# Feed-forward projections of a diffusion block: two plain matrix products against one Strassen level each

## The chip, the cores and the metric

One core of a Trainium2 chip (trn2) runs the whole layer as one program. The metric is device time in microseconds (us) of one execution, as the median of several runs. PE is the matmul engine (TensorE), DVE the vector engine, ACT the scalar engine, POOL is GpSimd, and SP is the engine whose queue issues most transfers.

## The reference

The layer mixes 1024 tokens of width 1024 (retention, Fourier mixing, gates) and ends in a gated feed-forward network with a width-3 depthwise convolution over the tokens, which is what changes here:

```python
x = x + g1 * y
h2 = modulate(rms_norm(x, norm2_w[layer]), sh2, sc2)
x = x + g2 * conv_ffn(h2, w_up[layer], conv_w[layer], conv_b[layer], w_down[layer])
...
def conv_ffn(h, w_up, conv_w, conv_b, w_down):
    u = depthwise_conv3(h @ w_up, conv_w, conv_b)
    a, val = jnp.split(u, 2, axis=-1)
    return (jax.nn.gelu(a) * val) @ w_down
```

`w_up` is 1024 x 5632, `w_down` 2816 x 1024, and all is float32; the result is `rms_norm(x, final_norm_w)`.

## The kernel before

Every large float32 product is done as three fast ones: `split` (L93) copies an operand rounded to the matmul's format into a "hi" tile on ACT and takes the rest into a "lo" tile with a subtraction on DVE, and `mm3` (L111) adds hi*hi, lo*hi and hi*lo (L112 to L114) into one PSUM tile. A PE instruction multiplies a 128 x 128 block by a 128 x 512 block.

The stage ahead of the feed-forward network takes tokens in two halves t = 0, 1 of 512. For each it makes `re` (retention projection, merged with the gates into `y`), then `wo` (output projection; two column halves i, four token blocks n), adds to the residual `acc`, sums squares on ACT (`sum_sq`, L740), takes the reciprocal root on POOL (`rms_rstd`, L743), and turns `acc` by PE transposes (L810) into `h2` with the features on the partitions. A small matmul `rb` (L804) spreads the root over the partitions; DVE scales the transposes with it.

The feed-forward loop runs over NF = 22 blocks i of 128 channels. Each loads its piece of `w_up` (`wload_k`), makes the two tiles `u` (gate and value, j = 0, 1) over all tokens with 2 x 2 x 8 x 3 = 96 matmuls, convolves (one ACT pass, L867, and two DVE passes of 1023 columns), applies gelu (L874), multiplies, and splits the product into `p`. After each second block `down(q)` multiplies that `p` by 256 rows of `w_down`, 96 matmuls again, and DVE adds the result to `acc` (L49). The last `down` also normalises and stores the output, token block by token block. `acc` stays in SBUF all through.

The order on each engine is not the program's order: the framework schedules it when the program is built (`schedule_with_timeline_sim=True`), and each engine then runs its list in that order, waiting where an operand is not there. Loads are issued by SP. PSUM has four kinds of tiles, of which `rt` and `mmt` hand out the ones used here.

Of the kernel before, what the change touches and what calls it, by code (L numbers as in the profile page):

```python
# [16 lines left out]
P = 128  # L17
# [8 lines left out]
NF = FF // P  # L26
EPS = 1e-6
# [15 lines left out]
def tile_block(ctx: ExitStack, tc: tile.TileContext, a: dict, out: bass.AP):  # L43
# [19 lines left out]
    wp = ctx.enter_context(tc.tile_pool(name="wp", bufs=2))  # L63
    ap = ctx.enter_context(tc.tile_pool(name="ap", bufs=4))
# [62 lines left out]
    pr = [ctx.enter_context(tc.tile_pool(name="pr0", bufs=2, space=PSUM))]  # L127
# [221 lines left out]
    with tc.tile_pool(name="rp", bufs=1) as rp:  # L349
# [173 lines left out]
        pm.append(ctx.enter_context(tc.tile_pool(name="pm", bufs=2, space=PSUM)))  # L523
        pr.append(ctx.enter_context(tc.tile_pool(name="pr1", bufs=2, space=PSUM)))
# [227 lines left out]
    with tc.tile_pool(name="mp", bufs=2) as mp, tc.tile_pool(name="bp", bufs=2) as bp:  # L752
        g1 = mp.tile([P, L], F32, tag="g1", bufs=1, name="g1")
        dma(g1, g_d[0].partition_broadcast(P))

        r = load_r(0)
        for t in range(2):
            y = tuple((ap if t == 0 else bp).tile([P, KD, 512], F32R, tag="A" if t == 0 else "B", name=f"y{t}{n}")
                      for n in "hl")
            for i in range(4):  # L760
                w = wload_k(a["w_ret"], i, f"wr{t}")
                sr = mp.tile([P, 2, 512], F32, tag="xn", bufs=4, name=f"sr{t}{i}")
                tf = mp.tile([P, 2, 512], F32, tag="xn", bufs=4, name=f"tf{t}{i}")
# [3 lines left out]
                ps = mmt(f"re{t}{i}").rearrange("p (m n) -> p m n", m=2)  # L767
                for j in range(2):
                    for k in range(KD):
                        mm3(ps[:, j, :], pick(w, ALL, k, blk(j)), pick(r, ALL, k), k == 0, k == KD - 1)  # L770
                for j in (slice(0, 2),) if i < 3 else (slice(0, 1), slice(1, 2)):
                    tt(sr[:, j], sr[:, j], ps[:, j], MUL)
                    tt(sr[:, j], sr[:, j], tf[:, j], ADD)
                    ys = slice(2 * i + j.start, 2 * i + j.stop)
                    split(y[0][:, ys, :], y[1][:, ys, :], sr[:, j])
            for n in range(4):
                dma(acc[t][:, n, :], a["xn"][4 * t + n])
            for i in range(2):
                pns = [rt(f"wo{t}{i}{n}") for n in range(4)]
                for q in range(2):  # L780
                    w = wload_k(a["w_out"], 2 * i + q, f"wo{t}{q}", 4)
                    for n in range(4):
                        for k in range(4):
                            mm3(pns[n], pick(y, ALL, 4 * q + k, blk(n)), pick(w, ALL, k), k + q == 0, k + q == 4)
                if t == 0 and i == 1:
                    r = load_r(1)
                if i == 1:
                    sqs = [ssq(f"b{t}{n}") for n in range(4)]
                    junk = mp.tile([P, L], F32, tag="xn", bufs=4, name=f"junk{t}")
                    for n in range(4):  # L790
# [8 lines left out]
            h2.append(tuple(ap.tile([P, KD, 512], F32R, tag="A", name=f"h2{t}{n}") for n in "hl"))
            dg = mp.tile([P, 4, P], F32, tag="dg", bufs=1, name=f"dg{t}")  # L800
            for n in range(4):
                tsc(dg[:, n, :], ident, rms_rstd(sqs[n]), MUL)
            ps = rt(f"rb{t}")
            T.matmul(ps, ones[:, 0:128], dg.rearrange("p n c -> p (n c)"), start=True, stop=True)  # L804
            rb = mp.tile([P, 512], F32, tag="rb", bufs=1, name=f"rb{t}")
            S.copy(rb, ps)
            for k in range(KD):
                ps = rt(f"tr{t}{k}")
                for n in range(4):
                    T.transpose(out=ps[:, blk(n)], in_=acc[t][:, n, blk(k)], identity=ident)  # L810
                hf = mp.tile([P, 512], F32, tag="rraw", bufs=2, name=f"h2f{t}{k}")
                hi, lo = h2[t][0][:, k, :], h2[t][1][:, k, :]
                stt(hf, ps, a2[:, k:k + 1], rb, MUL, MUL)
                S.activation(hi, hf, AF.Identity, bias=b2[:, k:k + 1])
                stt(lo, hf, b2[:, k:k + 1], hi.bitcast(F32), ADD, SUB)

    with tc.tile_pool(name="ff", bufs=2) as ff:
        g2 = ff.tile([P, L], F32, tag="g2", bufs=1, name="g2")
        fnw = ff.tile([P, L], F32, tag="fnw", bufs=1, name="fnw")
        dma(g2, g_d[1].partition_broadcast(P))  # L820
        dma(fnw, a["fnw"].partition_broadcast(P))
        pts = []

        def down(q):
            last = q == NF // 2 - 1
            w = wload_k(a["w_down"], q, "wd", 2, scale=g2)
            for n in range(NT):
# [22 lines left out]
        for i in range(NF):  # L850
# [28 lines left out]
            if i % 2 == 1:  # L879
                pts.append(pt)  # L880
                if i > 1:
                    down(i // 2 - 1)
# [113 lines left out]
```

## Time and profile before

| | |
|---|---|
| median of 3 runs | 1619.82 us (1619.3 to 1620.79) |
| the profiled execution: span, first to last instruction | 1617.7 us |
| PE busy | 1597.0 us (99%), 8206 instructions |
| DVE busy | 893.0 us (55%), 1556 instructions |
| ACT busy | 473.3 us (29%) |
| POOL busy | 33.9 us (2%) |
| transfers | 152.87 MB, mean 94 GB/s |

The profiled execution is known by its span alone, which is 2.1 us under the median of the runs; that difference is what lies around it. The `re` matmuls start at 705.8 us, the first `u` matmul at 884.6 us, and the last `down` matmul at 1607.0 us.

### The profile page before, as it was taken

The page shows a single profiled execution, that of the slowest core. Times are in us where ns is not written, and L with a number is a line of the kernel's source. Part 1 is how long each engine was busy: PE and PEld are TensorE (multiplying, and loading weights), DVE is VectorE, ACT ScalarE, POOL GpSimd, SP SyncE. Part 2 cuts the span into 40 slices and gives each one's busy share as a digit, 9 for nine tenths or more (in the row PEclk, how much of TensorE's full clock was granted, in tenths as well). Part 3 has the DMA queues.
Part 4 walks back from the last instruction along what each step waited for, and adds up shares of the span by engine and source line. Part 5 has one row for each costly group of instructions (what it writes and reads, how often), then busy time and mean ns, then how long its engine had stood idle before and what let it go on. Part 6 is the DMA issues. An engine that isn't in the chain of part 4 may idle for free.

```text
span 1617.7 us, 19863 instructions
## 1 busy us (share of the span) xinstructions
PE 1597.0 (99%) x8206; PEld 1344.2 (83%) x8206; DVE 893.0 (55%) x1556; ACT 473.3 (29%) x715; POOL 33.9 (2%) x40
## 2 busy tenths in 40 slices
PE   7999999999999999999999999999999999999997
PEld 4789989898888888888888888888888888888886
DVE  5586739476642642135675655555465454554656
ACT  6563131232412231122433431221212212212123
POOL 0000000000000000000000000000000000000002
PEclk9999999999999999999999999999999999999999
DMA  9234121123443322185542211110111102011102
GB/s 357 98 134 158 59 98 55 70 85 131 141 146 113 119 66 73 46 309 172 183 156 88 69 52 51 54 51 28 52 53 52 53 29 75 32 47 53 52 13 105
DMA packets 51019, 152.87 MB, mean 94 GB/s; under 512 B 6241, under 2 KB 10609, under 8 KB 50929
## 3 DMA queue, kind: packets, MB, share of 16 engines
q1 hardware_dynamic: 50928, 151.61, 27.5%
q8 instruction: 64, 1.05, 0.3%
q14 instruction: 27, 0.21, 0.0%
HBM read 134.77 MB, written 16.79 MB: 94 GB/s over the span
## 4 chain that ended last, share of the span: by engine, by line
PE 95%; DVE 3%; DMA 1%; ACT 0%; issue 0%; SPq 0%; DVEq 0%; POOLq 0%; POOL 0%
PE u L113 10%; PE u L114 10%; PE u L112 10%; PE d L114 5%; PE d L113 5%; PE d L112 5%; PE gr L114 2%; PE g L114 2%; PE gr L112 2%; PE re L112 2%; PE gr L113 2%; PE gf L112 2%; PE re L114 2%; PE re L113 2%; PE gf L114 2%; PE gf L113 2%
## 5 line engine op out<-in xcount | busy, mean ns | idle before, releaser
L49 DVE TENSOR_TENSOR acc<-acc,d 128x512 f32<-128x512 f32 x176 | 118.6, 683 | 89.1 <-PE d L114 88.5
L58 DVE SCALAR_TENSOR_TENSOR t<-u,convw,t 128x1023 f32<-128x1023 f32 (+2 forms) x90 | 112.8, 1255 | 36.7 <-ACT t L867 35.6
L175 DVE SCALAR_TENSOR_TENSOR mt<-mt,silrow 128x512 f32<-128x512 f32 x64 | 41.7, 688 | 58.3 <-DMA mt<-wmT 58.2
L867 ACT ACTIVATE t<-u,convb,convw 128x1024 f32<-128x1024 f32 (+1 forms) x45 | 53.3, 1187 | 61.9 <-PE u L114 61.9
L491 ACT ACTIVATE on<-o,nm,rst 128x128 f32<-128x128 f32 x64 | 24.0, 456 | 90.3 <-DVE nm L58 90.3
L874 ACT ACTIVATE t<-t 128x1024 f32<-128x1024 f32 x22 | 23.3, 1060 | 69.4 <-DVE t L58 69.4
L49 DVE TENSOR_TENSOR s<-s,fo 128x1024 f32<-128x1024 f32 x8 | 9.8, 1220 | 54.9 <-PE fo L114 43.0
L58 DVE SCALAR_TENSOR_TENSOR ss<-ss,sm,kv 64x128 f32<-64x128 f32 x112 | 38.0, 346 | 3.0
L484 DVE BATCH_NORM_STATS2 st<-o 128x6 f32<-128x128 f32 x64 | 14.2, 284 | 36.3 <-PE o L477 36.3
L49 DVE TENSOR_TENSOR rr<-ot,sg 128x512 f32<-128x512 f32 x16 | 11.0, 688 | 33.6 <-PE ot L495 33.6
L487 POOL TENSOR_TENSOR rst<-rst,mhalf 128x4 f32<-128x4 f32 x16 | 17.3, 1081 | 491.2 <-DVE rst L53 491.2
L49 DVE TENSOR_TENSOR t<-t,t 128x1024 f32<-128x1024 f32 x22 | 26.9, 1221 | 0.4
L476 PE MATMUL o<-v,pt 128*128 128x128 f32 x128 | 24.8, 275 | 0.0
L477 PE MATMUL o<-ss,qfb 128*128 128x128 f32 x128 | 24.7, 275 | 0.0
L561 ACT COPY qkr<-qk 128x1024 f32<-128x1024 f32 x6 | 6.1, 1014 | 57.7 <-PE qk L114 57.7
L583 ACT ACTIVATE s<-gf,bbg 128x1024 f32<-128x1024 f32 x8 | 8.9, 1113 | 46.5 <-PE gf L114 46.5
L49 DVE TENSOR_TENSOR sr<-sr,re 128x1024 f32<-128x1024 f32 (+1 forms) x10 | 9.9, 1006 | 22.4 <-PE re L114 18.0
L49 DVE TENSOR_TENSOR ro<-qkr,ropec 128x512 f32<-128x512 f32 x32 | 20.8, 682 | 1.6 <-ACT qkr L561 0.9
L476 PEld LDWEIGHTS o<-v,pt 128*128 128x128 f32 x128 | 20.1, 191 | 0.9
L49 DVE TENSOR_TENSOR qfb<-qT,tab 64x1024 f32<-64x1024 f32 x16 | 19.5, 1219 | 0.2
L58 DVE SCALAR_TENSOR_TENSOR ek<-ek,er 128x512 f32<-128x512 f32 (+2 forms) x36 | 19.0, 526 | 0.9
L477 PEld LDWEIGHTS o<-ss,qfb 128*128 128x128 f32 x128 | 19.4, 192 | 0.0
(1208 smaller groups left out, 5069.7 us busy)
## 6 DMA issues: line engine op xcount, KB each, us to landing
mt<-wmT SPq DMA_DIRECT2D x32, 512.0 KB, 3.3
xh<-xT SPq DMA_DIRECT2D x8, 512.0 KB, 7.4
r_d<-rr SPq DMA_DIRECT2D x16, 256.0 KB, 3.3
sr_d<-sr SPq DMA_DIRECT2D x8, 512.0 KB, 4.0
t_d<-s SPq DMA_DIRECT2D x8, 512.0 KB, 2.6
rraw<-r_d SPq DMA_DIRECT2D x8, 512.0 KB, 4.3
acc<-xn SPq DMA_DIRECT2D x8, 512.0 KB, 9.1
sr<-sr_d SPq DMA_DIRECT2D x8, 512.0 KB, 5.6
```

Source lines behind the costliest of these rows:

```text
L49: V.tensor_tensor(out=out, in0=in0, in1=in1, op=op)
L58: V.scalar_tensor_tensor(out=out, in0=in0, scalar=s, in1=in1, op0=op0, op1=op1)
L112: T.matmul(o, l[0], r[0], start=first, stop=False)
L113: T.matmul(o, l[0], r[1], start=False, stop=False)
L114: T.matmul(o, l[1], r[0], start=False, stop=last)
L175: V.scalar_tensor_tensor(out=raw[:, c], in0=raw[:, c], scalar=1.0, in1=silrow[:, c], op0=MUL, op1=MUL, accum_out=acc[:, h:h + 1])
L476: T.matmul(o[:, blk(n)], pt[:, n, :], vt[t][:, n, blk(i)], start=True, stop=False)
L477: T.matmul(o[:, blk(n)], qfb[i][:, blk(4 * t + n)], ss[i][:, 4 * t + n, :], start=False, stop=True)
L487: G.tensor_tensor(out=rs, in0=rs, in1=mhalf, op=ALU.pow)
L491: S.activation(on[:, n, :], o[:, blk(n)], AF.Identity, bias=nm[:, n:n + 1], scale=rs[:, n:n + 1])
L867: S.activation(tl[:, o:o + n], ps, AF.Identity, bias=convb[:, c:c + 1], scale=convw[:, c, 1:2])
L874: S.activation(u[0], u[0], AF.Gelu_apprx_tanh)
```

## The change

Each of the two projections becomes one level of Strassen's scheme (in Winograd's form): the operands are cut in 2 x 2 blocks, and seven block products with sums of blocks take the place of eight. For the up projection the blocks are token halves and feature halves of `h2` (`hops`: a11, a12, a22 and the sums s1 to s4) and of the weights (`wops`: b11, b21, b22 and the sums t1 to t4); for each i, `chain` makes a product of 12 matmuls. Products that share a sum add up in one PSUM tile (`x`, `y`, `z`), with copies to `ca`, `cv` in between. The gated product of two channel blocks j and j + 11 goes through four more sums (`sums`) and is stored to DRAM by transfers that POOL issues, seven of 256 KB for each pair. When all is up, the down projection reads them back: seven products of 11 steps, in each of which both operands are split and 12 matmuls done. `x` after the first residual goes to DRAM as well (`x2_d`) and comes back at the end. PSUM becomes one pool of eight tiles.

The core of the diff (the `wo` code around it is reordered, too):

```diff
+    def chain(ps, x, y, first):
+        for k in range(4):
+            for l, r in ((0, 0), (0, 1), (1, 0)):
+                T.matmul(ps, x[:, l, k], y[:, r, k], start=(first and k == 0 and l + r == 0), ...)
+    def wop(i, name, src):
+        t = fw.tile([P, 2, 4, P], F32R, tag="op", bufs=8, name=f"w{name}{i}")
+        split(t[:, 0], t[:, 1], src)
+    def up_first(i):
+        bank[i, "x"], bank[i, "z"] = rt(f"x{i}"), rt(f"z{i}")
+        chain(bank[i, "x"], wops[i, "b11"], hops["a11"], True)
+        chain(bank[i, "z"], wops[i, "b21"], hops["a12"], True)
...
+        def hops_out(t, n):
...
+                h1, s12 = xn(f"h1{n}", (KD, P)), xn(f"s12{n}", (2, 4, P))
+                dma(h1, h_d[n].rearrange("p (k c) -> p k c", k=KD))
+                s1, s2, s3, s4 = s12[:, 0], s12[:, 1], h1[:, 0:4], h1[:, 4:8]
+                tt(s3, s3, lo, SUB)
+                tt(s2, hi, s3, SUB)
+                hop("s2", s2)
+                tt(s1, lo, hi, ADD)
+                hop("s1", s1)
+                hop("s3", s3)
+                tt(s4, s4, s2, SUB)
+                hop("s4", s4)
+                hop("a22", hi)
...
+        def up_mm(i):
...
+            S.copy(ca[:, lo], x)
+            tt(ca[:, lo], ca[:, lo], z, ADD)
+            chain(x, wops[i, "t2"], hops["s2"], False)
+            S.copy(cv[:, lo], x)
+            chain(y, wops[i, "t1"], hops["s1"], True)
+            S.copy(cv[:, hi], y)
+            chain(x, wops[i, "t3"], hops["s3"], False)
+            tt(cv[:, hi], cv[:, hi], x, ADD)
+            chain(y, wops[i, "b22"], hops["s4"], False)
+            tt(cv[:, lo], cv[:, lo], y, ADD)
+            chain(x, wops[i, "t4"], hops["a22"], False)
+            S.copy(ca[:, hi], x)
...
+        def sums(j, pa, pb):
+            A11, A21, A12, A22 = pa[:, 0:512], pa[:, 512:], pb[:, 0:512], pb[:, 512:]
+            G.dma_start(p_d[0][j], A11)
+            G.dma_start(p_d[1][j], A12)
+            G.dma_start(p_d[6][j], A22)
+            s1, s2, s3 = (ff.tile([P, 512], F32, tag="s", bufs=2, name=f"s{q}_{j}") for q in range(1, 4))
+            tt(s1, A21, A22, ADD)
+            G.dma_start(p_d[3][j], s1)
+            tt(s2, s1, A11, SUB)
+            G.dma_start(p_d[2][j], s2)
+            tt(s3, A11, A21, SUB)
+            G.dma_start(p_d[4][j], s3)
+            tt(A12, A12, s2, SUB)
+            G.dma_start(p_d[5][j], A12)
...
+        for k in K:
+            step(Y, a_op(5, k), dop("ob", f"ob5{k}", raws[3, k]), False, N4)
```

On every engine the order is the same as before up to the `re` matmuls. After them it differs in three places that matter below.

PE, at the start of the feed-forward network. Before (`u` tiles of the first channel block; `rb1`, `tr1k` belong to the second token half):

```order
L112 MATMUL u01_7548<-h20h_6731,wu0hi_7485 128x512
L113 MATMUL u01_7548<-h20l_6732,wu0hi_7485 128x512
L114 MATMUL u01_7548<-h20h_6731,wu0lo_7486 128x512
L112 MATMUL u01_7548<-h20h_6731,wu0hi_7485 128x512
L804 MATMUL rb1_7400<-dg1_7383,ones_84 128x512
L810 MATMUL tr11_7413<-ident_66,acc1_6131 128x128 x4
L113 MATMUL u01_7548<-h20l_6732,wu0hi_7485 128x512
L114 MATMUL u01_7548<-h20h_6731,wu0lo_7486 128x512
L112 MATMUL u01_7548<-h20h_6731,wu0hi_7485 128x512
```

Now (`wb` and `wt` are weight operands, `trNM` transposes of token block N):

```order
L774 MATMUL z0_7686<-a12_6721,wb210_7490 128x512 x10
L774 MATMUL z1_7738<-a12_6721,wb211_7646 128x512 x2
L774 MATMUL x11_7711<-a11_6720,wb1111_7565 128x512 x10
L774 MATMUL z11_7712<-a12_6721,wb2111_7568 128x512 x10
L774 MATMUL x1_7737<-a11_6720,wb111_7643 128x512 x10
L774 MATMUL z1_7738<-a12_6721,wb211_7646 128x512 x10
L826 MATMUL tr130_7764<-ident_66,xr13_7636 128x128 x4
L826 MATMUL tr131_7773<-ident_66,xr13_7636 128x128 x4
L774 MATMUL x0_7685<-s2_7412,wt20_7811 128x512 x2
L774 MATMUL y0_7828<-s1_7413,wt10_7814 128x512 x2
L774 MATMUL x0_7685<-s2_7412,wt20_7811 128x512 x10
L774 MATMUL y0_7828<-s1_7413,wt10_7814 128x512 x10
```

Before, 48 matmuls on the first token half (`h20`) stood around `rb1` and the transposes. Now the 72 matmuls of `x`, `z` of three blocks stand ahead of the last transposes `tr130`, `tr131`, and what follows needs `s2`, `s1` of all tokens and `wt20`.

DVE at the same place. Before (`dg` makes the root's diagonal, `h21l` is the second half's lo part):

```order
L53 TENSOR_SCALAR dg1_7383<-ident_66,ssqb12_7358 128x128 [waits Pool_49]
L49 TENSOR_TENSOR wu1lo_7608<-wu1r1_7613,wu1hi_7607 128x1024 [waits DMAHW4_49,Activation_49]
L49 TENSOR_TENSOR ssqb13_7359<-ssqb13_7359 128x1 [waits Activation_49]
L55 TENSOR_SCALAR ssqb13_7359<-ssqb13_7359 128x1 [waits DVE_49]
L53 TENSOR_SCALAR dg1_7383<-ident_66,ssqb13_7359 128x128 [waits Pool_49]
L58 SCALAR_TENSOR_TENSOR h2f10_7409<-tr10_7404,a2_78,rb1_7402 128x512 [waits Activation_49]
L58 SCALAR_TENSOR_TENSOR h2f11_7418<-tr11_7413,a2_78,rb1_7402 128x512 [waits PE_49]
L58 SCALAR_TENSOR_TENSOR h21l_7382<-h2f10_7409,modc_72,h21h_7381 128x512 [waits Activation_49]
L58 SCALAR_TENSOR_TENSOR h21l_7382<-h2f11_7418,modc_72,h21h_7381 128x512 [waits Activation_49]
```

Now (`s123`, `h13` are the sums of the last token block, `t1_0` to `t4_0` the weight sums of block 0):

```order
L50 TENSOR_TENSOR s123_7783<-hv13_7763,h13_7782 128x512 [waits DVE_49]
L50 TENSOR_TENSOR s1_7413<-s123_7783,s1_7413 128x4x128 [waits Activation_49]
L50 TENSOR_TENSOR s3_7414<-h13_7782,s3_7414 128x4x128 [waits Activation_49]
L50 TENSOR_TENSOR h13_7782<-h13_7782,s123_7783 128x512 [waits DVE_49]
L50 TENSOR_TENSOR s2_7412<-s123_7783,s2_7412 128x4x128 [waits Activation_49]
L50 TENSOR_TENSOR s4_7415<-h13_7782,s4_7415 128x4x128 [waits Activation_49]
L50 TENSOR_TENSOR t1_0_7805<-u0r1_7803,u0r0_7485 128x512 [waits DMAHW2_49]
L50 TENSOR_TENSOR ca0_7829<-ca0_7829,z0_7686 128x512 [waits Activation_49]
L50 TENSOR_TENSOR t2_0_7806<-u0r1_7803,t1_0_7805 128x512 [waits DVE_49]
L50 TENSOR_TENSOR t3_0_7807<-u0r1_7803 128x512
L50 TENSOR_TENSOR t4_0_7808<-u0r0_7485,t2_0_7806 128x512 [waits DVE_49]
L50 TENSOR_TENSOR wt20_7811<-t2_0_7806,wt20_7811 128x512 [waits Activation_49]
```

From the first column scaling of `hv10` to `wt20` there are 72 DVE instructions: 52 of 512 columns, 16 of 128 columns and 4 of one column. Two scalings and two subtractions for each of eight feature blocks stood in their place.

DVE at the end of the up loop. Before (the last gated product beside `down`'s additions):

```order
L49 TENSOR_TENSOR t210_11350<-t210_11350,t211_11403 128x1024 [waits DVE_49]
L49 TENSOR_TENSOR acc0_6130<-acc0_6130,d930_11471 128x512 [waits PE_49]
L49 TENSOR_TENSOR acc0_6130<-acc0_6130,d931_11479 128x512 [waits PE_49]
L49 TENSOR_TENSOR p20l_11288<-t210_11350,p20h_11287 128x1024 [waits Activation_49]
L49 TENSOR_TENSOR acc1_6131<-acc1_6131,d940_11487 128x512 [waits PE_49]
L49 TENSOR_TENSOR acc1_6131<-acc1_6131,d941_11495 128x512 [waits PE_49]
L49 TENSOR_TENSOR acc1_6131<-acc1_6131,d950_11503 128x512 [waits PE_49]
```

Now (`t210`, `t211` are the last block's tiles, `oa04`, `ob04` the first operands of the down products that are not prepared ahead), and under it ACT at the same place:

```order
L59 SCALAR_TENSOR_TENSOR t210_10913<-ca21_10822,convw_80,t210_10913 128x1023 [waits DMASW7_49,Activation_49]
L59 SCALAR_TENSOR_TENSOR t211_10917<-cv21_10823,convw_80,t211_10917 128x1023 [waits DMASW4_49,DMASW1_49,Activation_49]
L59 SCALAR_TENSOR_TENSOR t210_10913<-ca21_10822,convw_80,t210_10913 128x1023 [waits DVE_49]
L59 SCALAR_TENSOR_TENSOR t211_10917<-cv21_10823,convw_80,t211_10917 128x1023 [waits DVE_49]
L50 TENSOR_TENSOR t210_10913<-t210_10913,t211_10917 128x1024 [waits DVE_49,Activation_49]
L50 TENSOR_TENSOR s1_10_10926<-t100_10811,t210_10913 128x512 [waits DMASW3_49,DVE_49]
L50 TENSOR_TENSOR s2_10_10927<-s1_10_10926,t100_10811 128x512 [waits DMASW5_49,DVE_49]
L50 TENSOR_TENSOR t210_10913<-t210_10913,s2_10_10927 128x512 [waits DMASW7_49,DVE_49]
L50 TENSOR_TENSOR s3_10_10928<-t100_10811 128x512 [waits DMASW1_49]
L50 TENSOR_TENSOR oa04_10944<-pr04_10966,oa04_10944 128x512 [waits DMAHW6_49,Activation_49]
L50 TENSOR_TENSOR ob04_10963<-d0_4_10945,ob04_10963 128x512 [waits DMAHW7_49,Activation_49]
```

```order
L944 COPY ca21_10822<-x21_10760 128x512 [waits PE_49]
L952 ACTIVATE t210_10913<-ca21_10822,convb_81,convw_80 128x1024 [waits DMASW7_49,Activation_49]
L952 ACTIVATE t211_10917<-cv21_10823,convb_81,convw_80 128x1024 [waits DMASW4_49,DMASW1_49,DVE_49]
L956 ACTIVATE t210_10913<-t210_10913 128x1024 [waits DVE_49,Activation_49]
L97 CAST oa04_10944<-pr04_10966 128x512 [waits DMAHW6_49]
L97 CAST ob04_10963<-d0_4_10945 128x512 [waits DMAHW7_49]
```

The splits of `oa04`, `ob04` stand behind the whole last convolution, on ACT behind its gelu, and on DVE also behind two instructions that wait for stores (the DMASW waits).

## Rows read from the trace of the kernel before

**Rows 1.** The page: span, PE's busy time, the chain's shares by engine.

```profile
span 1617.7 us, 19863 instructions
...
PE 1597.0 (99%) x8206; PEld 1344.2 (83%) x8206; DVE 893.0 (55%) x1556; ACT 473.3 (29%) x715; POOL 33.9 (2%) x40
...
PE 95%; DVE 3%; DMA 1%; ACT 0%; issue 0%; SPq 0%; DVEq 0%; POOLq 0%; POOL 0%
```

**Rows 2.** Windows: us; busy us (instructions) of PE, PEld, DVE, ACT, POOL; clock; DMA.

```profile
885.00:1600.00 715.00, 715.00 (x3170) 592.12 (x3169) 389.49 (x423) 175.95 (x183) 3.15 (x5) 1.00 0.15 48
...
1200.00:1300.00 100.00, 100.00 (x443) 82.84 (x442) 51.04 (x50) 25.57 (x24) 0.00 (x0) 1.00 0.16 53
```

**Rows 3.** Timeline of DVE in the loop: start us, us, what.

```profile
1043.63 0.68 DVE L49 TENSOR_TENSOR acc<-acc,d 128x512 f32<-128x512 f32 x1
1044.23 1.22 DVE L49 TENSOR_TENSOR wu6lo<-wu6r,wu6hi 128x1024 fp32r<-128x1024 f32 x1
1045.36 0.68 DVE L49 TENSOR_TENSOR acc<-acc,d 128x512 f32<-128x512 f32 x1
1045.96 1.28 DVE L58 SCALAR_TENSOR_TENSOR t<-u,convw,t 128x1023 f32<-128x1023 f32 x1
1047.15 1.27 DVE L49 TENSOR_TENSOR acc<-acc,d 128x512 f32<-128x512 f32 x2
```

**Rows 4.** Timeline, the norm of one token block (`wo`, t = 1), all engines.

```profile
877.25 0.68 DVE L49 TENSOR_TENSOR xt<-wo,g 128x512 f32<-128x512 f32 x1
...
877.96 0.69 DVE L49 TENSOR_TENSOR acc<-acc,xt 128x512 f32<-128x512 f32 x1
...
878.69 0.60 ACT L741 ACTIVATE wo<-acc 128x512 f32<-128x512 f32 x1 [2.80 <-DVE acc L49]
...
880.88 0.54 POOL L746 TENSOR_TENSOR ssqb<-ssqb,mhalf 128x1 f32<-128x1 f32 x1 [82.07 <-DVE ssqb L55]
...
881.45 0.29 DVE L53 TENSOR_SCALAR dg<-ident,ssqb 128x128 f32<-128x128 f32 x1 [0.65 <-POOL ssqb L746]
```

**Rows 5.** ACT by line and form: count, busy us, mean ns, idle before.

```profile
L867 ACT ACTIVATE t<-u,convb,convw 128x1024 f32<-128x1024 f32 x43 | 51.9, 1206 | 60.2 <-PE u L114 60.2
L491 ACT ACTIVATE on<-o,nm,rst 128x128 f32<-128x128 f32 x64 | 24.0, 456 | 90.3 <-DVE nm L58 90.3
L874 ACT ACTIVATE t<-t 128x1024 f32<-128x1024 f32 x22 | 23.3, 1060 | 69.4 <-DVE t L58 69.4
...
L844 ACT ACTIVATE out<-acc,ssqf 128x1024 f32<-128x1024 f32 x2 | 2.3, 1150 | 0.0
```

**Rows 6.** Timeline of PE: the root's matmul and four transposes.

```profile
893.90 1.02 PE L804 MATMUL rb<-dg,ones 128*128 128x512 f32 x2
894.76 0.60 PE L810 MATMUL tr<-ident,acc 128*128 128x128 f32 x4
```

**Rows 7.** Transfers: GB/s in 40 slices; issues with KB and us to landing.

```profile
GB/s 357 98 134 158 59 98 55 70 85 131 141 146 113 119 66 73 46 309 172 183 156 88 69 52 51 54 51 28 52 53 52 53 29 75 32 47 53 52 13 105
...
r_d<-rr SPq DMA_DIRECT2D x16, 256.0 KB, 3.3
...
m_4r<-wm SPq DMA_DIRECT2D x2, 512.0 KB, 11.6
```

**Rows 8.** Timeline of the end, all engines.

```profile
1606.96 0.39 PE L114 MATMUL d<-wd10hi,p20l 128*128 128x512 f32 x1
...
1608.62 3.50 DVE L58 SCALAR_TENSOR_TENSOR out<-acc,ssqf,fnw 128x512 f32<-128x512 f32 x2
1608.71 2.86 POOL L845 TENSOR_TENSOR out<-out,fnw 128x1024 f32<-128x1024 f32 x1
...
1613.10 1.41 DVE L58 SCALAR_TENSOR_TENSOR out<-acc,ssqf,fnw 128x512 f32<-128x512 f32 x2 [0.72 <-POOL ssqf L746]
```

**Rows 9.** Windows: the stretch after the last matmul.

```profile
1610.00:1617.70 7.70, 0.00 (x0) 0.00 (x0) 3.75 (x5) 0.00 (x0) 2.11 (x2) 0.67 0.53 204
```

More of the change, by code (lines that the diff above doesn't have):

```diff
@@ L26 @@
 NF = FF // P
+NH = NF // 2
 EPS = 1e-6
@@ L750, in ssq @@
         return const.tile([P, 2], F32, tag="ssq", bufs=8, name=f"ssq{name}")
-    with tc.tile_pool(name="mp", bufs=2) as mp, tc.tile_pool(name="bp", bufs=2) as bp:
+    hops = {}
+    order = [j + NH * e for j in range(NH) for e in range(2)]
+    wops = {}
+    bank = {}
+    def chain(ps, x, y, first):
+        for k in range(4):
+            for l, r in ((0, 0), (0, 1), (1, 0)):
+                T.matmul(ps, x[:, l, k], y[:, r, k], start=(first and k == 0 and l + r == 0),
+                         stop=(k == 3 and l == 1), skip_group_check=True)
@@ L773, in tile_block @@
+                    tt(sr[:, j], sr[:, j], ps, MUL)
                     tt(sr[:, j], sr[:, j], tf[:, j], ADD)
-                    ys = slice(2 * i + j.start, 2 * i + j.stop)
-                    split(y[0][:, ys, :], y[1][:, ys, :], sr[:, j])
+                    split(y[0][:, 2 * i + j, :], y[1][:, 2 * i + j, :], sr[:, j])
+                    if t == 1 and i < 2:
+                        hops_out(0, 2 * i + j)
+            acc = [mp.tile([P, L], F32, tag="acc", bufs=4, name=f"acc{4 * t + n}") for n in range(4)]
@@ L799, in tile_block @@
[L799 to L815, printed above, removed]
@@ new lines, in tile_block @@
+            if t == 0:
+                r = load_r(1)
+                hops["a11"], hops["a12"] = pair(ap, "a11"), pair(ap, "a12")
+            else:
+                wps.close()
+                fw = ops.enter_context(tc.tile_pool(name="fw", bufs=1, side="right", reuse_waits="tile"))
+                for n, pool in (("s2", bp), ("s1", ap), ("s3", ap), ("s4", bp), ("a22", bp)):
+                    hops[n] = pair(pool, n)
+            for n in range(4):
+                ps = rt(f"wo{t}1{n}")
+                for q in range(2):
+                    wo_mm(ps, y, ws[q], q, n)
+                wo_out(ps, acc[n][:, 512:], 1, sqs[n])
+                norm(t, n, acc[n], sqs[n])
+                if t == 1:
+                    if n > 0:
+                        up_prep0(order[n - 1])
+                    if n > 0:
+                        hops_out(t, n - 1)
@@ L875, in tile_block @@
             tt(u[0], u[0], u[1], MUL)
[L876 to L883 removed]
+            return u[0]
+        def sums(j, pa, pb):
[12 more added lines that the diff above has]
+            G.dma_start(p_d[5][j], A12)
@@ new lines, in down_first @@
+        def down_first(k):
+            raw = fw.tile([P, 2, 512], F32, tag="raw", bufs=3, name=f"d0raw{k}")
+            dma(raw[:, 0], p_d[0][k])
+            dma(raw[:, 1], a["w_down"][0, k])
+            if k % 2 == 0:
+                first.append(ap.tile([P, 2, 4, 512], F32R, tag="A", name=f"first{k}"))
+            op = first[k // 2][:, k % 2]
+            split(op[:, 0:2], op[:, 2:4], raw)
+        first = []
+        up_prep(order[0])
+        for n, i in enumerate(order):
+            cs = up_mm(i)
+            if n + 1 < NF:
+                if n > 1:
+                    up_prep0(order[n + 1])
+                    up_first(order[n + 1])
+                up_prep(order[n + 1])
+            else:
+                for k in range(4):
+                    down_first(k)
+            p = conv(i, *cs)
+            if n % 2 == 0:
+                pa = p
+            else:
+                sums(n // 2, pa, p)
```

318 lines of the change are left out of this document (221 added, 97 removed).

## The prediction

> **What bounds the kernel now.** I read the page first: PE is busy 99% of the span, and 95% of the chain that ended last is PE's [rows 1]. An engine that full sets the time, so next I asked whether that holds in the stretch that changes. The windows say so: from 885 to 1600 us, the whole feed-forward network, PE has no idle time at all at the full clock (a granted 1.00, the 2.4 GHz level), while DVE is busy 389 of 715 us and ACT 176 [rows 2]. The reader should take two things from it. A matmul removed here is worth its full time: 443 instructions in 100 us, or 0.2257 us each. And DVE has only half of its time left, which is what a scheme that buys matmuls with additions spends.
>
> **What is removed.** Up: each of 22 channel blocks needs 7 products x 12 = 84 matmuls in place of 96, so 264 fewer. Down: 7 x 11 x 12 = 924 in place of 1056, so 132 fewer. 396 x 0.2257 = **-89.4 us**. The `rb` matmuls go too, four of them; two in a row take 0.86 us to the transposes behind them [rows 6], so **-1.7**. The transposes stay at 64.
>
> **The up loop.** PE now needs 84 x 0.2257 = 19.0 us for one channel block. What DVE must do in that time, counted in the order: 7 splits, 4 weight sums, 3 additions from PSUM and half of the pair's 4 sums make 16 passes of 512 columns; to these come 4 convolution passes and 1 product of 1024 columns. Passes that don't wait for each other start 0.60 us apart, though the row says 0.68 long, the convolution 1.19, the 1024-column pass 1.13 [rows 3]; one that needs the result before it starts 0.71 later [rows 4]. I take 0.64: 16 x 0.64 + 4 x 1.19 + 1.13 = 16.1 us, 85% of 19.0. ACT has 11 copies and casts near 0.6, two convolution passes of 1.21 and a gelu of 1.06 [rows 4, 5]: 10 us. So PE stays the bound, with 2 x (19.0 - 16.1) = 5.7 us of slack for a pair of blocks. The operand pool holds eight weight operands, seven chains of lead, which hides the bunches. For what it doesn't hide I take **+4** over the loop; the ends are 0 and, if half of a block's slack of 2.9 showed as idle time, 22 x 1.4 = 30.
>
> **The boundary into the up projection** is the largest price. Before, 48 matmuls on the first token half hid the second half's norm. Now three blocks' `x` and `z` chains (72 matmuls) do it; 24 of them are all that remains once the last transposes wait. Set the clock to 0 where `wo`'s second column half starts. Its 48 matmuls end at 10.9. Block 0 of the second token half is finished at 9.5; its norm chain takes from 877.25 to 881.45, 4.2 us with a wait behind other work, some 3.2 without [rows 4], then a scaled copy of 1024 columns, 1.15 [rows 5]. Its transposes can go near 14.2. From there DVE runs 72 instructions in order up to `wt20`, the operand that the first chain behind the transposes needs: 52 x 0.64 = 33.3; 16 of 128 columns at 0.29 [rows 4], 4.8; four small ones, 0.6. Each block's scaling alternates with copies on ACT (0.46 for 128 columns [rows 5]), of which some 2.4 in all shows, and waits for its `h1` load and the norms I put at 3. So `wt20` is there at about 60. PE's work up to that point is 168 matmuls, 37.9, and 32 transposes at 0.11 (four pass in 0.60, 0.1 of it the last one's end [rows 6]), 3.5: 41.4. The loss is **+19**. If the unchained price of 0.60 held and the alternation cost nothing, about 8.5; with 0.71 for each, 24.
>
> **The boundary into the down projection.** At its own zero `y21`'s last chain ends; PE still has 42 matmuls, 9.5 us: the rest of `x21` (12, to 5.2 with other work between) and products of the down steps prepared ahead. The splits of `oa04`, `ob04` stand behind the last block's whole convolution, as the order shows. Copy of `x21` to 6.0; ACT's two passes of 1.21 to 8.3; four DVE passes to 12.1; product to 13.4; `s1`, `s2` to 14.9. `A12` may then be overwritten only when its store has landed, and `s3` takes the buffer of `s1`, whose store is the third of its queue. The trace has no transfer that POOL issues; the nearest row, 256 KB out through SP, lands in 3.3 us [rows 7]. That gives `s3` at 19.2 and the splits near 20. PE waits about **+10** (5 if the stores land at once, 15 if they take twice as long). Loads behind it: about 15.7 MB in the first 61 us of the down projection, 257 GB/s, where one slice of 40 us shows 309 [rows 7].
>
> **The rest.** In an idle stretch the granted clock falls: behind the last matmul the window shows 0.67 [rows 9]. Two stretches of idle will show the 1.2 GHz level for some microseconds at their end: **+3**, an estimate (0 to 8). In the last down product DVE has about 33 us of work beside PE's 132 x 0.2257 = 29.8: **+2** (0 to 15 over the down projection). The end: before, the last matmul ends at 1607.2 and the span at 1617.7, 10.5 us, with one block's work left. Now four blocks are finished behind the last matmuls: four scalings, four additions, eight output halves, 16 DVE passes x 0.67 = 10.7, with norms in the gaps, and 3.2 to the end as from 1614.5 now [rows 8]: 13.9, **+3.4**. Work ahead of `wo` has the same order as before: 0.
>
> **The sum** against the profiled execution: 1617.7 - 89.4 - 1.7 + 4 + 19 + 10 + 3 + 2 + 3.4 = 1568.0; the median of the runs is 2.1 above its span, so **1570 us**. With the bounds of these terms, not all at one end, 1555 to 1592.
>
> POOL's stores deserve the weighing. The row of 3.3 us [rows 7] belongs to another queue, so it bounds from one side only. The Trainium skill ("SBUF — State Buffer", section "SBUF: two separate sides") says that a transfer issued from GpSimd needs descriptors which GpSimd writes, and that a DVE operation in its two-port mode locks it out: some 620 ns alone against 3100 overlapped. By it, an estimate from that page, each store would land 2.5 us later, both waits together would cost a pair under 5 us, less than the loop's slack, and only the second boundary would grow, by some 5 us, to 1575. No row here shows such a transfer.
>
> **The rivals.** *Hidden boundaries, 1530 to 1555.* Both waits stay near their lower ends, because DVE's passes go at 0.60 and the scaled copies overlap: 1617.7 - 91.1 + 8.5 + 5 + 3.4 + 2.1 = 1545.6. For it: the loop's rows show the short spacing. Against it: the order shows the 72 instructions behind each other, many on the one before.
>
> *The up loop is bound by DVE, 1592 to 1616.* POOL issues seven stores for each pair, and POOL and DVE slow each other: the same two output halves take 3.50 us beside 2.86 us of POOL and 1.41 without [rows 8], 0.73 us lost for each us of POOL. An issue of 1 us would cost a pair 5.1, inside the slack of 5.7; at 1.5 us it is 7.7, 2.0 over, x 11 = +22. Against it: POOL's row reads SBUF data, an issue moves none.
>
> *Stores that land late, over 1623: the other side.* In each pair two DVE instructions wait in order for a store (`A12` minus `s2`, and `s3`), and behind them on DVE stand the next blocks' weight sums, splits and the additions that free PSUM; PE stops when these stop. Between a store's issue and the waiting instruction DVE has about 3.4 and 4.0 us of its own work (by its order, at the prices above). To eat the gain, 1620 - 1570 = 50 us over 11 pairs, each pair must lose 4.5 on top of the slack of 5.7, 10.2 over two waits: from a landing time of about 8.6 us on the change is slower. At 12 us the two waits are 8.6 and 8.0, 11 x (16.6 - 5.7) = +120. For it: a load of 512 KB took 11.6 us when the queues were full [rows 7]. Against it: the loop moves 50 GB/s, and the 3.3 us is for the same size.
>
> **Chances.** Forecast 0.56, hidden boundaries 0.20, DVE bound 0.15, late stores and slower 0.06, within 0.2% 0.03; 0.2%, 3.2 us, is about what a measurement of this kernel tells from no change. Faster is the first three: 0.91. The range of 1542 to 1608 leaves out the lower part of the hidden case (some 0.06), and above it a third of the DVE case and the last two (0.14).
>
> **What would show it.** Right: PE idle some 15 to 20 us between the last transposes and `x0`'s chain on `s2`; some 10 us ahead of the matmuls on `oa04`; none to speak of between, with 19.0 us for a block; granted clock under 1.00 only at these two places and the end; stores near 3 us from issue to landing; 14 us behind the last matmul. Wrong: a gap of PE in each pair, with DVE waiting for a store before `A12` or `s3` (late stores), or DVE passes of 512 columns well over 0.7 us beside POOL's issues (DVE bound).

## The result, and where the time went

The changed kernel takes **1593.48 us** (1592.96 to 1595.7) against 1620.3 beside it: a ratio of 0.9837, with an interval of 0.9823 to 0.9851. It is 27 us faster; 50 were forecast. The time lies inside the stated range of 1542 to 1608, and some 23 us of the gain are missing.

The page of the changed kernel, for [rows 1]:

```profile
span 1591.8 us, 20417 instructions
...
PE 1536.5 (97%) x7806; PEld 1275.2 (80%) x7806; DVE 1032.2 (65%) x1920; ACT 630.0 (40%) x1084; POOL 70.6 (4%) x115
...
PE 84%; DVE 8%; DMA 5%; ACT 1%; issue 1%; SPq 0%; POOL 0%; DVEq 0%; ACTq 0%; POOLq 0%
```

PE has its 400 instructions less (7806 against 8206), but is busy only 60.5 us less, where the prediction priced the 400 at 91.1. Its share of the chain fell from 95% to 84%; DVE has 8% in place of 3, and transfers 5% in place of 1, of which 3 are loads of `mt` between 230 and 470 us, in stages ahead of the change. The windows of the changed stages, columns as in [rows 2]:

```profile
870.00:950.00 80.00, 63.48 (x259) 50.16 (x258) 56.30 (x101) 40.28 (x76) 3.14 (x4) 0.85 0.29 99
950.00:1340.00 390.00, 390.00 (x1679) 316.02 (x1678) 321.41 (x424) 190.50 (x283) 37.41 (x70) 1.00 0.30 104
1360.00:1400.00 40.00, 31.68 (x128) 25.11 (x127) 28.80 (x42) 17.92 (x30) 3.21 (x6) 0.87 0.87 318
1400.00:1450.00 50.00, 48.77 (x215) 39.84 (x214) 42.01 (x67) 21.86 (x40) 0.00 (x0) 1.00 0.66 232
1450.00:1570.00 120.00, 120.00 (x531) 99.34 (x531) 79.48 (x134) 57.51 (x109) 2.97 (x4) 1.00 0.35 109
```

Read them for two things. First the idle time of PE: 80 - 63.48 = 16.5 us around the entry to the up projection, none in the 390 us of its loop, 8.3 + 1.2 at the entry to the down projection. The waits of PE say for whom (total, times, longest):

```profile
PE x L774 <- ACT wt L97: 10.1, 1, 10.1
...
PE dx L1017 <- DVE ob L50: 4.8, 1, 4.8
PE tr L826 <- ACT xr L818: 3.6, 1, 3.6
PE dx L1017 <- ACT ob L97: 3.5, 1, 3.5
...
PE x L774 <- DVE acc L50: 2.0, 1, 2.0
...
PE dy L1017 <- ACT oa L97: 1.2, 1, 1.2
...
PE x L774 <- ACT wb L97: 0.9, 1, 0.9
```

The second boundary, 4.8, 3.5 and 1.2 us, is where the forecast put it. At the first, only 10.1 us lie where it looked for 15 to 20, between the last transposes and the chain on `s2`; 3.6 us come before the first transposes (`tr` waits for `xr`), 2.0 and 0.9 before the first chains. Second, the count: in the up loop PE never waits, at a granted clock of 1.00, and still passes only 1679 instructions in 390 us, 0.2323 us each. In the down projection it is 531 in 120 us, 0.2260, the pace of before. (A window also counts the matmuls under way at its edges: the 443 in 100 us that the prediction read as 0.2257 us each start 0.2267 apart, which is 0.4 us on all that were removed.) The slow pace is not the loop's own. It is there in the `re` stage, whose matmuls and their order are the same in both kernels (the kernel before, then the changed one):

```profile
710.00:780.00 70.00, 70.00 (x311) 57.95 (x310) 35.85 (x37) 22.22 (x28) 0.00 (x0) 1.00 0.62 219
```

```profile
710.00:780.00 70.00, 70.00 (x303) 56.75 (x302) 33.65 (x41) 15.58 (x21) 0.00 (x0) 1.00 0.59 203
```

311 matmuls against 303 in the same 70 us without idle time. From the starts of neighbouring matmuls over the whole trace: 4253 of them, all but 23 ahead of 1362 us, where the up projection ends, start 0.2275 to 0.245 us after the one before, and together lose 24.5 us against 0.2267. Before the change 523 do and lose 2.9, scattered but for the Fourier stage's `fo` matmuls, 190 of 192. The difference, **21.6 us**, is what the forecast lacked.

What distinguishes these matmuls is where their operands lie. One line of the diff that looked like housekeeping moves the weight pool to the other end of SBUF:

```diff
-    wp = ctx.enter_context(tc.tile_pool(name="wp", bufs=2))
+    wp = wps.enter_context(tc.tile_pool(name="wp", bufs=2, side="right"))
```

By the addresses in the built program (no trace has them), the weight tiles stood at 24416 bytes and upwards, the activations at 85856: both are 96 modulo 256. Now the weights of `re` stand at 184288, which is 224 modulo 256, and the activations at 40800, still 96. The operands of a matmul are 128 bytes apart, modulo 256. In the down projection both come from one pool again, and are 0 apart. And the `fo` matmuls that were slow before had tiles (175072 and 135008) 128 apart, where those of the `gf` matmuls around them (24416 and 69472), at full pace, were 0 apart. It is so in every stage of 512-column matmuls: before the change all but `fo` are 0 apart, after it all but the down projection are 128 apart. That made a theory that could be tried without touching any engine's order.

### The profile page after: what moved, and what is told of

The parts are those of the page before. It is cut to its first block, busy times and chain, and to the rows that moved or that the text cites. A ratio compares the mean times of both kernels' runs of the same rounds, so it can differ in the third digit from the quotient of the medians.

```text
span 1591.8 us, 20417 instructions
## 1 busy us (share of the span) xinstructions
PE 1536.5 (97%) x7806; PEld 1275.2 (80%) x7806; DVE 1032.2 (65%) x1920; ACT 630.0 (40%) x1084; POOL 70.6 (4%) x115
## 4 chain that ended last, share of the span: by engine, by line
PE 84%; DVE 8%; DMA 5%; ACT 1%; issue 1%; SPq 0%; POOL 0%; DVEq 0%; ACTq 0%; POOLq 0%
PE x L774 16%; PE y L774 8%; PE dx L1017 7%; PE z L774 4%; DMA mt<-wmT 3%; PE dy L1017 2%; PE dz L1017 2%; PE wo L116 2%; PE wo L115 2%; PE gf L115 2%; PE re L117 2%; PE re L115 2%; PE wo L117 2%; PE g L117 2%; PE re L116 2%; PE gf L117 2%
## 5 line engine op out<-in xcount | busy, mean ns | idle before, releaser
L774 PE MATMUL x<-s,wt 128*128 128x512 f32 x528 | 133.0, 397 | 10.1 <-ACT wt L97 10.1
L774 PEld LDWEIGHTS x<-s,wt 128*128 128x128 f32 x528 | 100.0, 190 | 34.3 <-ACT wt L97 10.3
L1017 PE MATMUL dx<-ob,oa 128*128 128x512 f32 x480 | 112.5, 396 | 8.3 <-DVE ob L50 4.8
L1017 PEld LDWEIGHTS dx<-ob,oa 128*128 128x128 f32 x480 | 91.5, 191 | 28.6 <-DVE ob L50 5.5
L774 PE MATMUL x<-a,wb 128*128 128x512 f32 x264 | 67.7, 403 | 2.9 <-DVE acc L50 2.0
L774 PE MATMUL z<-a,wb 128*128 128x512 f32 x264 | 70.0, 399 | 0.0
L774 PE MATMUL y<-s,wt 128*128 128x512 f32 x264 | 67.1, 397 | 0.0
L774 PE MATMUL y<-s,wb 128*128 128x512 f32 x264 | 65.2, 395 | 0.0
L774 PE MATMUL x<-a,wt 128*128 128x512 f32 x264 | 65.0, 395 | 0.0
L1017 PE MATMUL dy<-ob,oa 128*128 128x512 f32 x264 | 60.8, 390 | 1.2 <-ACT oa L97 1.2
L774 PEld LDWEIGHTS y<-s,wt 128*128 128x128 f32 x264 | 50.0, 189 | 11.6
L1017 PEld LDWEIGHTS dy<-ob,oa 128*128 128x128 f32 x264 | 49.4, 188 | 12.1 <-ACT oa L97 1.6
L774 PEld LDWEIGHTS y<-s,wb 128*128 128x128 f32 x264 | 49.7, 188 | 11.6
```

Of the source, the lines that this page charges most:

```text
L774: T.matmul(ps, x[:, l, k], y[:, r, k], start=(first and k == 0 and l + r == 0), stop=(k == 3 and l == 1), skip_group_check=True)
L1017: T.matmul(ps[n], x[l][:, blk(n)], y[r], start=(first and l + r == 0), stop=(l == 1), skip_group_check=True)
```

## Experiments on the distance of the operands

A pad moves tiles and nothing else: in all runs of this section but the last, which gives up a buffer, PE runs the same matmuls in the same order as the kernel that the run comes from.

**A pad of 128 bytes in the changed kernel.**

```diff
+    padp = ctx.enter_context(tc.tile_pool(name="padp", bufs=1, side="right"))
+    padp.tile([P, 32], F32, name="pad")
     wps = ctx.enter_context(ExitStack())
```

> The changed kernel with 128 unused bytes per partition at the top of SBUF, ahead of the weight pools; the order of every engine stays as it is. Theory: a 512-column matmul starts 0.2324 us after the one before instead of 0.2267 wherever the tile that PE loads and the tile that it streams stand 128 bytes apart (modulo 256), which the change brought about by moving the weight pool to the other end of SBUF. The pad takes the 128 bytes away: the spacing in the up loop and in the stages ahead of it falls to 0.2267, the 4253 slow matmuls lose 24.5 us less 2.9 for those that were slow before too, and the time is about 1572 (1570 to 1576, as some waits don't shrink). Rival: the slow spacing belongs to the program as a whole (its POOL transfers, busier DVE and ACT, the chip of that run): no change, 1593, spacing 0.232.

Measured: 1575.13 us (1573.97 to 1576.19), ratio 0.9717 to the kernel before (0.9702 to 0.9731). Of the 21.6 us, 18.4 came back; where the other 3 went was not traced. **A pad of 64 bytes** (16 in place of 32):

> The same pad with 64 bytes: the two operands then stand 64 bytes apart. If any distance that is not a multiple of 256 slows the matmul: about 1593, spacing 0.232. If it takes a distance of 128: about 1572, spacing 0.2267. Rival (program as a whole): 1593 as well.

Measured: 1592.8 us, the median of two runs, 1589.53 and 1596.08. **The kernel before, activations moved by 128 bytes** (the same two lines, without `side`, between `wp` and `ap`):

> The kernel before with 128 unused bytes between the weight pool and the pools of the activations, so that only the latter move. Theory (distance of the two operands): the spacing becomes 0.2324 from the first stage to the end, some 5100 matmuls x 0.0057 = 29 us: about 1649. Rival, absolute address of one of the tiles (some start at 224 modulo 256): also about 1649. Rival, program as a whole: 1620.

Measured: 1649.63 us (1648.05 to 1651.01), ratio 1.018 (1.0163 to 1.0196). **The kernel before, both moved** (the lines ahead of `wp`):

> The kernel before with the 128 bytes ahead of the weight pool, so that both kinds of tiles move and their distance stays. Theory (distance): 1620, spacing 0.2267. Rival, absolute address: 1649, spacing 0.2324.

Measured: 1620.79 us, ratio 1.000 (0.9991 to 1.001). **A pad of 96 bytes in the changed kernel**:

> The changed kernel with a pad of 96 bytes, so that the loaded and the streamed tile of a matmul stand 32 bytes apart (modulo 256) instead of 128. If every distance but 0 slows the matmul: spacing 0.232 to 0.233 in the up loop, 430 to 432 instructions in 100 us, about 1593. If only multiples of 64 do: 443 and 1575.

Measured, in a single run: 1597.18 us. **The kernel before, activations moved by 256 bytes**:

> The kernel before with 256 unused bytes between the weight pool and the activations' pools; to make room two raw weight buffers stand in place of three, which may move loads. If the distance counts modulo 256: spacing 0.2267, 443 instructions in 100 us, about 1620. If it counts modulo 512 or more: 0.232, 432 instructions, about 1649.

Measured, in a single run: 1623.9 us. The same window of all six traces, in this order (changed kernel with 128, 64, 96; before with activations moved by 128, both by 128, activations by 256):

```profile
1200.00:1300.00 100.00, 100.00 (x443) 82.84 (x442) 84.59 (x114) 48.76 (x74) 10.81 (x20) 1.00 0.33 111
```

```profile
1200.00:1300.00 100.00, 100.00 (x430) 80.60 (x429) 81.31 (x108) 46.80 (x70) 10.81 (x20) 1.00 0.31 104
```

```profile
1200.00:1300.00 100.00, 100.00 (x430) 80.54 (x429) 80.46 (x108) 47.34 (x71) 9.19 (x17) 1.00 0.28 98
```

```profile
1200.00:1300.00 100.00, 100.00 (x432) 80.91 (x431) 49.46 (x54) 19.94 (x19) 0.00 (x0) 1.00 0.13 42
```

```profile
1200.00:1300.00 100.00, 100.00 (x443) 82.81 (x442) 51.74 (x51) 25.57 (x24) 0.00 (x0) 1.00 0.16 53
```

```profile
1200.00:1300.00 100.00, 100.00 (x443) 82.84 (x442) 54.05 (x54) 24.51 (x23) 0.00 (x0) 1.00 0.16 53
```

The instruction count of PE, first in parentheses, is all that has to be read: 443 where the distance is 0 modulo 256 (or exactly 256), 430 to 432 where it is 32, 64 or 128. PE is without idle time at clock 1.00 in all six. So the rivals fall. It is not the program as a whole, since a pad that nobody reads or writes gives 18 us back. It is not the busier DVE: with the pad DVE is busy 84 of 100 us and the pace is full, and in the old kernel with moved activations it is busy 49 and the pace is slow. It is not the absolute address: with both moved the time stays. What counts is the distance of the loaded tile from the streamed one, modulo 256 as far as 0, 32, 64, 128 and 256 show it; which of the two is weight and which activation does not matter (in `re` the weights are loaded, in `wo` the activations, and both stages were slow). Why the array pays for it was not tried. The Trainium skill ("TensorE: Matmul & The Clock Gate", "Part 2: What happens when you issue a matmul") says that loading the next weights doesn't steal SBUF read bandwidth from the running matmul, as the two are read through independent ports; here the pace depends on where the two lie to each other, 443 against 430 to 432 instructions in 100 us, so that can't be all.

## Experiments on the boundaries

All of these stand on the changed kernel with the pad, 1575.13 us. Unlike a pad, each of these edits makes the framework order the engines anew, so more moves than the edit itself, and the runs of one version lie 2 to 6 us apart.

**The last transposes earlier:**

```diff
-        for i in order[:3]:
+        for i in order[:2]:
             up_first(i)
         hops_out(1, 3)
+        up_first(order[2])
```

> All four of this batch stand on the changed kernel with the pad of 128 bytes, 1575 us. Here the transposes of the last token block stand ahead of the x and z chains of the third channel block instead of behind them, so 24 matmuls (5.4 us) follow the transposes. Theory (first boundary): PE's 10.1 us of idle ahead of the chain on s2 is the time from the transposes through DVE's sums and splits to wt20; with cover behind the transposes it falls to 5 or 6, and the time to 1570 or 1571. Rival: DVE's 72 instructions set the end by their own number, whenever the transposes come: within 1 us of 1575.

Measured: 1571.0 us (1567.58 to 1571.95). PE's wait for `wt` fell as expected; the two `dx` waits of the second boundary moved as well, from 4.5 and 3.5 us:

```profile
PE x L776 <- ACT wt L99: 5.7, 1, 5.7
PE dx L1020 <- DVE ob L50: 5.3, 1, 5.3
...
PE dx L1020 <- ACT ob L99: 1.3, 1, 1.3
```

Cover behind the transposes counts, not DVE's number of instructions alone; but DVE's work then still ends 5.7 us too late.

**Six prepared steps in place of four** (`down_first` and the tests on `k` with 6 for 4):

> Six steps of the first down product are prepared ahead of the last convolution in place of four. Theory (second boundary): PE's two waits of 3.5 and 4.5 us for oa04, ob04 and the next step are there because those splits stand behind the whole last convolution; 24 more matmuls of cover (5.4 us) take about 5 us away: 1570. Rival: the wait is for transfers (loads of p_d and w_down, stores of the last pair), and the same idle comes 5.4 us later: 1575.

Measured: 1578.17 us (1575.71 to 1579.24), not faster than the 1575.13 of the base. The waits of the down projection (`dx`, `dy`) with four and with six prepared steps:

```profile
PE dx L1019 <- DVE ob L50: 4.5, 1, 4.5
...
PE dx L1019 <- ACT ob L99: 3.5, 1, 3.5
...
PE dy L1019 <- ACT oa L99: 1.2, 1, 1.2
```

```profile
PE dx L1019 <- ACT ob L99: 4.5, 1, 4.5
...
PE dy L1019 <- DVE ob L50: 2.9, 3, 1.2
PE dx L1019 <- ACT oa L99: 2.5, 1, 2.5
```

The first wait is shorter, 4.5 against 8.0 us, and the rest came back as waits for the next operands: 9.9 in all, against 9.2. In this version the loads of the steps behind went out only from 1354.9 us on, after the last product, where they had gone out from 1338.7 with four steps; `ob` waited for its load of `w_down`:

```profile
1354.93 0.33 SPq L1030 DMA_DIRECT2D d<-w_down  x1
...
1358.69 0.62 ACT L99 CAST ob<-d 128x512 fp32r<-128x512 f32 x1 [6.26 <-DMA d<-w_down]
```

The rival had it right: cover alone doesn't help where the loads start later for it.

**Sums in place:**

```diff
-            tt(s3, A11, A21, SUB)
-            G.dma_start(p_d[4][j], s3)
-            tt(A12, A12, s2, SUB)
-            G.dma_start(p_d[5][j], A12)
+            tt(A21, A11, A21, SUB)
+            G.dma_start(p_d[4][j], A21)
+            tt(A11, A12, s2, SUB)
+            G.dma_start(p_d[5][j], A11)
```

> The third sum goes in place into A21 and the new A12 into A11, whose stores have landed long ago, so no DVE instruction of sums waits for a store of its own pair. Theory: the two waits (1.65 and 0.49 us at the last pair) are worth about 2 us at the second boundary and nothing in the loop, where PE has no idle time: 1573. Rival of the prediction (stores that land late cost time in each pair): 11 pairs x 2 us, 1553.

Measured: 1570.38 us (1566.05 to 1571.17), 4.7 under the base: more than the 2 of the theory, far from the 22 of the rival. The `dx` waits fell from 8.0 to 4.6 (3.1 for DVE and 1.5 for ACT), so 3.4 of it is seen there. Not all of that is the sums, because the order at the end of the loop changed, too. Matmuls of the prepared steps behind the last chain of `x`, in the base and here:

```profile
1343.36 4.47 PE L1019 MATMUL dx<-first 128*128 128x512 f32 x19
```

```profile
1340.27 6.51 PE L1019 MATMUL dx<-first 128*128 128x512 f32 x28
```

The nine more cover 2.0 us, which is what the wait for ACT lost (3.5 to 1.5). The version with the transposes earlier serves for comparison: it has 29 matmuls there and the old sums, and its `dx` waits are 1.3 and 5.3 us. Against it the sums in place take 2.0 us off these two waits, the 2 of the theory; the rest of the 4.7 can't be told from the new order, which also moved the waits of `dy` (3.0 us there, 1.2 here and in the base).

**Stores through SP in place of POOL** (`dma` for `G.dma_start` in `sums`):

> The seven stores of each pair are issued by SP in place of POOL. Theory: POOL's issues (0.54 us each, 2.7 us to landing) cost the loop nothing, and the landing through SP is about the same: within 2 us of 1575. Rival (POOL's issues and DVE slow each other, or stores through POOL land late for it): faster by some 5 us, most of it at the second boundary. Against it: SP would then wait for DVE in order ahead of its weight loads, which could cost some us.

Measured: 1576.68 us (1574.46 to 1580.48), no difference that the runs can tell. But the objection came true in the trace. PE's wait, and the load and the cast of `oa` that end it:

```profile
PE dx L1019 <- ACT ob L99: 10.9, 1, 10.9
```

```profile
1357.17 0.38 SPq L1013 DMA_DIRECT2D pr<-p_d  x1
...
1359.99 0.62 ACT L99 CAST oa<-pr 128x512 fp32r<-128x512 f32 x1 [8.75 <-DMA pr<-p_d]
```

The load went out behind the last pair's stores in SP's queue, some 17 us after the last chain of `y`, where it goes out right after that chain when POOL issues the stores. PE's waits at the second boundary are 12.1 us in all, against 9.2. So this run does not part the two sides: what the stores gained there (DVE waits 0.67 and 0.62 us for them, in place of 1.65 and 0.49), the loads behind them lost.

**The best version: pad, transposes and sums together.**

> The pad of 128 bytes, the transposes of the last token block ahead of the third block's x and z chains, and the sums in place, together. Theory: the three act in different stages and add up: 1575.1 - 4.1 (transposes) - 4.7 (sums) = 1566. Rival: what one of them saves comes back as a wait of the down projection's first loads, as in the run with six prepared steps: 1570.

Measured: **1567.19 us** (1566.05 to 1568.72), ratio 0.9677 (0.9661 to 0.9693) to the kernel before, and 26 us under the changed kernel. That is nearer to the theory's 1566 than to the rival's 1570, though the two lie hardly further apart than its runs. PE's wait for `wt` is 8.2 us here and 5.7 with the transposes alone, and still nothing is lost by it. From the first transposes to the chain on `s2`, with the transposes alone and then here:

```profile
882.37:929.02 46.65, 36.48 (x152) 29.41 (x152) 37.09 (x71) 26.85 (x52) 2.06 (x2) 0.83 0.33 114
```

```profile
880.87:924.67 43.80, 32.03 (x152) 25.48 (x152) 36.74 (x71) 26.52 (x52) 2.06 (x2) 0.95 0.34 121
```

The chain came 2.9 us sooner. PE did its 152 instructions in 32.0 us in place of 36.5, at a granted clock of 0.95 in place of 0.83, and so stood waiting longer for DVE, which is busy some 37 us in both. Part of this version's gain lies in that clock, at which neither edit was aimed.

## Why the prediction was right in part

The forecast was 49.8 us under the kernel before by its own sum; 26.8 came. By number alone, 1593 lies just above the forecast's own bounds (1555 to 1592) and in the rival of the DVE-bound loop (1592 to 1616), whose mechanism the trace doesn't show; that the stated range held it is in part luck. Term by term, measured in the trace of the changed kernel against [rows 1]:

| term | forecast | measured |
|---|---|---|
| matmuls removed | -91.1 | -91.1 at the prediction's price: 400 instructions less; 443 in 100 us return with the pad |
| pace of the remaining matmuls | 0 | **+21.6** |
| up loop | +4 | 0: 390 of 390 us busy |
| entry to the up projection | +19 | +16.5 of idle time |
| entry to the down projection, and its supply | +10, +2 | +9.5 |
| clock at its lower level | +3 | +7.4 |
| end | +3.4 | +3.9: 14.3 us from PE's last end to the span's |
| ahead of `wo` | 0 | +4.7 of idle time |

The measured terms sum to -27.5, the span shrank by 25.9; 1.6 are not placed. (Clock: 44 matmuls between 870 and 1440 us start 0.25 to 0.5 us after the one before, 7.4 us over 0.2267; 5.1 of it lie at the first entry, where the clock fell to the 1.2 GHz level three times, in or right behind the waits of 3.6, 2.0 and 10.1 us, while the forecast counted one such stretch there. Ahead of `wo`: PE's idle time up to 870 us, 15.1 us against 10.4; its cause was not tried. With the pad it is 14.6, and single executions of the other versions show 11.6 to 13.6 for the kernel before and 12.3 to 17.3 for the changed one, so part of the 4.7 is spread.)

**The step that failed** is "Work ahead of `wo` has the same order as before: 0", and with it the price of 0.2257 us for every matmul that stays. The order was indeed the same; the tiles had moved, and a matmul's price is not a property of its order. With the distance put right, the kernel is at 1575.13, 5 us from the forecast of 1570, so the other terms stand together, some because their errors cancel: the clock cost twice its estimate, the loop nothing. (Two slips in the prediction change no term: the `wo` half whose "48 matmuls end at 10.9" has 96, of which these are the first two token blocks', and its 168 counts all; and by its own terms late stores eat the gain from a landing time of 8.8 us on, not 8.6.)

The boundary into the up projection cost nearly what was forecast, but not in the way that was worked out. Transposes, the wait, and the first chain on `s2` in the timeline of PE; below it DVE's last scalings of `hv`, and its splits of `wt`:

```profile
929.28 1.03 PE L826 MATMUL tr<-ident,xr 128*128 128x128 f32 x8
940.42 1.22 PE L774 MATMUL x<-s,wt 128*128 128x512 f32 x2 [10.10 <-ACT wt L97]
...
930.41 1.78 DVE L56 TENSOR_SCALAR hv<-tr,a,modc 128x128 f32<-128x128 f32 x4 [3.22 <-ACT hv L832]
...
940.83 1.89 DVE L50 TENSOR_TENSOR wt<-t,wt 128x512 fp32r<-128x512 f32 x3
```

And the window from DVE's first scaling to the split of `wt20`, columns as in [rows 2]:

```profile
891.80:940.83 49.03, 36.08 (x147) 28.47 (x146) 38.06 (x71) 26.35 (x51) 2.06 (x2) 0.81 0.28 97
```

The prediction let DVE run its 72 instructions nearly without a break, to 60 us after the start of `wo`'s second column half, and PE be done with its own work at 41.4. From the same start, 875.2, the chain on `s2` came at 65.2. DVE's work was as forecast, 38.1 us busy (38.7), in passes that start 0.60 apart at the last token block, as in [rows 3]; but it stood idle for 11.0 us, where 5.4 had been allowed. Of that, 3.2 are its wait for the last transposes, which stand behind 72 matmuls on PE, and the run with the transposes earlier gave 4.1 us back. PE's own work took 48.7 us, 7.3 more than forecast, 5.1 of it the clock and 1.0 the slow pace. Two errors, 5 us later for DVE and 7 for PE, leave 16.5 of idle time near the forecast's 19: the size is in part luck.

The boundary into the down projection, ACT and DVE on one line of time:

```profile
1367.36 1.06 ACT L956 ACTIVATE t<-t 128x1024 f32<-128x1024 f32 x1 [2.67 <-DVE t L59]
1368.32 0.60 ACT L97 CAST oa<-pr 128x512 fp32r<-128x512 f32 x1
...
1369.49 0.97 PEld L1017 LDWEIGHTS dx<-ob,oa 128*128 128x128 f32 x4 [3.92 <-ACT ob L97]
...
1372.77 0.69 DVE L50 TENSOR_TENSOR t<-t,s 128x512 f32<-128x512 f32 x1 [1.53 <-DMA p_d<-t]
...
1374.05 0.69 DVE L50 TENSOR_TENSOR s<-t 128x512 f32<-128x512 f32 x1 [0.59 <-DMA p_d<-s]
1374.66 0.68 DVE L50 TENSOR_TENSOR oa<-pr,oa 128x512 fp32r<-128x512 f32 x1
...
1376.00 2.21 PEld L1017 LDWEIGHTS dx<-ob,oa 128*128 128x128 f32 x6 [5.54 <-DVE ob L50]
```

The cast of `oa` waits behind the gelu; the four hi*hi matmuls run; two DVE instructions wait 1.53 and 0.59 us for stores, and the split of `oa` comes at 1374.66, 18.3 us behind the end of `y`'s chain (1356.35), where some 20 had been worked out. This boundary went as worked out.

The rivals. *Hidden boundaries*: no, both waits are there, though DVE's passes did go at the 0.60 us on which this rival rested. *DVE-bound loop*: no; PE has no idle time in it, and 512-column passes of DVE stay at 0.69 us beside POOL's issues of 0.54. *Late stores*: no; PE has no gap in the pairs, and the stores landed sooner than the nearest row of before (3.3 us [rows 7]) said:

```profile
pr<-p_d SPq DMA_DIRECT2D x73, 256.0 KB, 2.6
...
p_d<-t POOLq DMA_DIRECT2D x44, 256.0 KB, 2.6
...
p_d<-s POOLq DMA_DIRECT2D x33, 256.0 KB, 3.1
```

The Trainium skill ("SBUF — State Buffer", section "SBUF: two separate sides") was weighed as 2.5 us more for each store, since DVE can keep GpSimd from writing descriptors. With DVE 82% busy in the loop, the stores landed in 2.6 and 3.1 us here, with the pad in 2.7 and 2.9, and through SP, on the same base, in 2.4 and 2.2:

```profile
p_d<-t SPq DMA_DIRECT2D x44, 256.0 KB, 2.4
...
p_d<-s SPq DMA_DIRECT2D x33, 256.0 KB, 2.2
```

That is 0.3 to 0.7 us more through POOL, not 2.5, and the measurement decides. Whether DVE's passes here ran in the two-port mode of which that page speaks, no run shows.

## What to carry to other kernels

Compare a stage that the change does not touch before looking at the ones that it does: 311 against 303 matmuls in the same window without idle time said that the price of all matmuls had changed. When pools move, look at the distance of each matmul's two SBUF operands modulo 256 bytes; 128 unused bytes were worth 18 us here. And cover for a wait is worth something only if the loads behind it start no later: the two prepared steps more gave nothing, and taking waits away (sums in place) did. Last, an edit can make the framework order everything anew, so before a gain is put down to it, compare the order around the place: nine matmuls that moved were as much as the edit here.

## What was not expected of the hardware

A 128 x 512 matmul passes every 0.2267 us when its loaded and its streamed tile lie a multiple of 256 bytes apart (0 and 256 were run), and every 0.2324 to 0.2333 at 32, 64 and 128: 2.5 to 2.9%, at a granted clock of 1.00 and with nothing in the waits to show it. PE counts as busy all the time; only the count of instructions in a window tells. In the slow case the spacing is not even: with a distance of 128 it runs through seven steps of 0.228 to 0.241 us and begins again, and with 32 and 64 it alternates between 0.231 and 0.235 or so. Why was not tried.
